# Gates stored 32 tokens at a time, picks made first, small transfers by way of DRAM, the last modulation column one pair behind its load

## The chip, the cores and the metric

The kernel runs on one NeuronCore of a Trainium2 chip. The metric is the device time of one execution in microseconds, the median of several runs. TensorE multiplies matrices, VectorE (DVE) and ScalarE (ACT) work element by element, GpSimd (POOL) mainly issues gathers here, and SyncE (SP) issues the other transfers. Each engine takes its instructions in order. An instruction that waits for a transfer holds up all that stand behind it on its engine, and the same holds for the queue of transfers that an engine issues.

## What is computed

One layer of a diffusion backbone over 512 tokens of width 1024. A token mixer of two gated scans comes first. Then comes a retrieval layer, cut here to its core:

```python
q = (t @ w_query).reshape(PEER_BLOCK, PEER_HEADS, 2, PEER_DQ // 2)
s1 = jnp.einsum('thd,nd->thn', q[:, :, 0], k1)
s2 = jnp.einsum('thd,nd->thn', q[:, :, 1], k2)
v1, i1 = lax.top_k(s1, PEER_TOPK)
v2, i2 = lax.top_k(s2, PEER_TOPK)
...
top_s, pos = lax.top_k(cand_s, PEER_TOPK)
idx = jnp.take_along_axis(cand_i, pos, axis=-1)
g = jax.nn.softmax(top_s, axis=-1)
act = jax.nn.gelu(jnp.einsum('thkd,td->thk', expert_u[idx], t))
return jnp.einsum('thk,thkd->td', (g * act), expert_v[idx])
```

For each token, 8 heads pick 16 of 16384 experts each. An expert is one row of U and one row of V. The result times a modulation vector g2 = silu(c) @ w_ada + b, plus the residual, is normalised and written.

## The kernel before

**Two ways to the same sum.** Tokens stand in four blocks of 128. For block 3 the picked rows are fetched with indirect gathers (tile erow, `fetched`, L1199): 128 rows of U, multiplied with h on VectorE (L1229), and 128 rows of V, added up in yg (L1242). For blocks 0 to 2 (384 tokens) the kernel computes all 16384 experts densely: `hidden` (L1138) makes gelu(U h) for one pair of 128 experts at a time, 64 pairs in all, `gated` (L1162) multiplies by a gate matrix that is zero where an expert was not picked, and `combine` (L1189) adds the pair's V rows into six accumulators y. The last 16 tokens of the 384 are left out of `hidden` (368 columns instead of 384); their products come from 16 more fetched rows, the s rows (L1223), whose sums sdots go through a gelu (L1225) and are put into the tile act by eight small transfers (L1227).

**Float32 in three products.** Each operand is split into a high and a low part: ScalarE writes the high part (uh, vh, ah; L1134, L1181), VectorE the rest (ul, vl, al; L1135, L1182), and TensorE runs three matmuls for each (`mm3`, L139 to L141). The tile pH holds `hidden`, y `combine`, pG the gates. A pair's `combine` is 36 matmuls of 512 columns, its `hidden` 48 of 368. V rows (tile vr, 1 MB a pair) are loaded and split by `load_split` (L1125), U rows (ur) too.

**The gate matrix.** `gate_block` (L1114) builds gates for 8 tokens at a time, 48 groups: VectorE makes one-hot factors (L1093 to L1104), TensorE multiplies them (pG, L1110), ScalarE copies them into the tile stage (L1111), and when 16 tokens are full SP stores the stage to Gd in DRAM (L1121), 24 stores of 1 MB. `gated` reads Gd back for four pairs at a time into Gn (L1169, 1.5 MB).

**Order.** The queries come first and with them the picks, four blocks of `picks` (L1022), then the gate stage with `hidden` and fetched rows mixed in; the constants ROWS say how many fetched rows go with each gate group, with each half of a pair that has `hidden`, and with each half of one that has none. By the end of the gate stage 32 pairs of `hidden` are asked for, so the main loop has 32 pairs with `hidden` and `combine`, then 29 with `combine` alone, and a tail of three. The gelus of 28 pairs are kept in DRAM (Hd, stored at L1155, loaded back at L1161). When the last `hidden` is done its memory is freed for a new pool, `vring`. From there on the V rows of pairs alternate between the two pools, and `mods_last` (L251) runs: it loads silr once (L255) and eight columns wg of the g2 weights (L259), each followed by a product on VectorE (L260), one per pair.

VectorE's order within the loops is settled by the scheduler when the program is built, from the order of the code and its estimates of when inputs are ready.

Of the kernel before, what the change touches and what calls it, by code (L numbers as in the profile page):

```python
# [19 lines left out]
D = 1024  # L20
# [11 lines left out]
class Net:  # L32
# [218 lines left out]
    def mods_last(self, pool):  # L251
# [680 lines left out]
class Peer:  # L932
# [10 lines left out]
    GT = 16  # L943
# [4 lines left out]
    ROWS = (0.85, 2.85, 0.83)  # L948
# [73 lines left out]
    def picks(self, w, b):  # L1022
# [12 lines left out]
        for s in range(2):  # L1035
# [11 lines left out]
        key = self.key = (self.n.q0[0][:, 256:512].rearrange("p (s h k) -> p s h k", s=2, h=8) if b == 2 else  # L1047
                          w.tile([128, 2, 8, 16], F32, name="key"))
# [114 lines left out]
    def gated(self, n, pool, vpool, bufs, mark=None, home=None):  # L1163

        nc = self.nc
        NG, NU = self.TD // self.GT, self.TU // self.GT
        if 2 * n % self.GN == 0:
            self.Gn = pool.tile([128, NG, self.GN, self.GT], F32, name="Gn", bufs=2)
            nc.sync.dma_start(self.Gn, self.Gd[:, :, 2 * n:2 * n + self.GN, :].rearrange("g m n t -> m g n t"))  # L1169
# [4 lines left out]
        nc.scalar.activation(g4[:, :, NU:], gates[:, :, NU:], AF.Copy)  # L1174
        with self.tc.issue_after(mark) if mark else ExitStack():
            nc.vector.tensor_tensor(g4[:, :, :NU], g4[:, :, :NU], gates[:, :, :NU], op=OP.mult)
# [20 lines left out]
    def fetched(self, w, ring, y):  # L1197
# [64 lines left out]
    def run(self, es, out):  # L1262
# [5 lines left out]
        self.Hd = dp.tile([self.SPILL, 128, 2, self.TU], F32, name="Hd")  # L1268
        kept, out_to = self.AHEAD, self.AHEAD + self.SPILL
        seq = [*range(kept), *range(out_to, 64), *range(kept, out_to)]  # L1270
        self.shared = False
        self.gel, self.last = {}, 2 * seq[-1]
# [5 lines left out]
        with ExitStack() as e0:  # L1278
# [5 lines left out]
            with ExitStack() as e1:  # L1284
                w = e1.enter_context(tc.tile_pool(name="top", bufs=1, side="right", reuse_waits="tile"))
# [5 lines left out]
                self.iota2 = w.tile([128, 128, 2], BF, name="iota2")  # L1291
# [8 lines left out]
                with tc.tile_pool(name="wq", bufs=1, reuse_waits="tile") as wp:  # L1300
# [10 lines left out]
                    nc.gpsimd.tensor_copy(self.iota2, n.iota_row[:, :, None].to_broadcast([128, 128, 2]))  # L1311
# [6 lines left out]
                self.ixs = fp.tile([128, self.SH], I32, name="ixs")  # L1318
                self.dots, self.act = (n.q0[0][:, i:i + 128] for i in (0, 128))
# [3 lines left out]
                def index():  # L1323
# [149 lines left out]
```

## Time and profile before

| | us |
|---|---|
| runs of the kernel | 1751.51, 1754.22, 1760.5; median 1754.22 |
| profiled execution | 1756.08, of it 1754.0 in the span |
| TensorE, VectorE, ScalarE, GpSimd busy | 1666.8, 1449.4, 830.5, 500.1 |
| gate matmuls (pG), first to last start | 689.6 to 923.3 |
| combine matmuls (y), first start | 948.5 |
| mean granted clock of TensorE | 0.98 of full speed |

A matmul's modelled duration overlaps the next one's, so TensorE can be "busy" nearly all the time without running at its peak. A better measure is the number of matmuls that start in a window, set against the shortest steady distance between two. The granted clock shows in windows where TensorE had to wait.

### The profile page before, as it was taken

The numbers are of one execution on the slowest core, as the hardware profiler recorded it, in microseconds if no ns is written. First come the engines' busy times: TensorE is split into PE (matmuls) and PEld (weight loads), VectorE is DVE, ScalarE is ACT, GpSimd is POOL, SyncE is SP. The second block draws the span as 40 slices with busy tenths as digits, with TensorE's granted clock in tenths as the row PEclk, the third lists the DMA queues.
The fourth block names the chain that finished last, engine by engine and source line by source line (L and its number), as shares of the span: only waits on it lengthen the run. The fifth ranks groups of instructions, "written<-read, shape, count | busy, mean of one in ns | idle before, by whom it ended". The sixth has DMA issues, their size and how long they took to land. (4 is left out here: it accounts for less than half of the span.)

```text
span 1754.0 us, 27581 instructions
## 1 busy us (share of the span) xinstructions
PE 1666.8 (95%) x10440; PEld 1456.8 (83%) x10440; DVE 1449.4 (83%) x2824; ACT 830.5 (47%) x1413; POOL 500.1 (29%) x327
## 2 busy tenths in 40 slices
PE   6999999989999999989998999999999998999995
PEld 3888877877788999988997989999999997788884
DVE  6688988877989999979996698788778876778677
ACT  4667677655233365757663244333333332234231
POOL 0000000000043012212383575565556551323310
PEclk8999999989999999999999999999999999999998
DMA  8345445133322247878899989999999989999962
GB/s 315 128 145 160 131 144 181 55 156 136 146 85 73 97 155 272 323 265 295 334 324 384 363 338 360 348 329 348 352 319 355 345 282 346 329 321 336 327 214 96
DMA packets 155687, 439.13 MB, mean 250 GB/s; under 512 B 13105, under 2 KB 69777, under 8 KB 135074
## 3 DMA queue, kind: packets, MB, share of 16 engines
q1 hardware_dynamic: 114322, 289.94, 47.7%
q0 software_dynamic: 40400, 145.34, 22.7%
q8 instruction: 81, 1.33, 0.3%
q10 hardware_dynamic: 832, 2.11, 0.3%
q14 instruction: 52, 0.43, 0.1%
HBM read 388.93 MB, written 48.39 MB: 249 GB/s over the span
## 5 line engine op out<-in xcount | busy, mean ns | idle before, releaser
L141 PE MATMUL pH<-hh,ul 128*128 128x368 f32 x1024 | 340.9, 333 | 4.0 <-DVE ul L1135 4.0
L139 PE MATMUL pH<-hh,uh 128*128 128x368 f32 x1024 | 340.4, 332 | 3.2 <-ACT gels L1153 2.5
L140 PE MATMUL pH<-hl,uh 128*128 128x368 f32 x1024 | 338.1, 330 | 0.0
L139 PE MATMUL y<-vh,ah 128*128 128x512 f32 x756 | 297.0, 394 | 13.2 <-ACT ah L1181 7.2
L1214 POOL DMA_INDIRECT erow<-in_v_dram,ix x128 | 231.2, 1806 | 255.8 <-DVE yg L1242 168.0
L141 PE MATMUL y<-vh,al 128*128 128x512 f32 x756 | 295.8, 392 | 3.6 <-DVE al L1182 3.6
L140 PE MATMUL y<-vl,ah 128*128 128x512 f32 x756 | 296.8, 393 | 0.1
L1214 POOL DMA_INDIRECT erow<-in_u_dram,ix x128 | 202.6, 1583 | 254.6 <-DVE erow L1229 141.9
L1134 ACT ACTIVATE uh<-ur 128x1024 fp32r<-128x1024 f32 x128 | 135.3, 1059 | 209.6 <-PE pH L140 181.4
L1135 DVE TENSOR_TENSOR vl<-vr,vh 128x1024 fp32r<-128x1024 f32 x126 | 153.3, 1222 | 95.6 <-ACT vh L1134 95.5
L1134 ACT ACTIVATE vh<-vr 128x1024 fp32r<-128x1024 f32 x126 | 132.4, 1055 | 186.8 <-PE y L141 128.0
L139 PEld LDWEIGHTS pH<-hh,uh 128*128 128x128 f32 x1024 | 193.2, 189 | 5.3 <-ACT gels L1153 2.8
L141 PEld LDWEIGHTS pH<-hh,ul 128*128 128x128 f32 x1024 | 193.0, 189 | 5.4 <-DVE ul L1135 5.4
L140 PEld LDWEIGHTS pH<-hl,uh 128*128 128x128 f32 x1024 | 193.3, 189 | 1.3
L139 PEld LDWEIGHTS y<-vh,ah 128*128 128x128 f32 x756 | 143.7, 190 | 43.6 <-ACT ah L1181 8.5
L1135 DVE TENSOR_TENSOR ul<-ur,uh 128x1024 fp32r<-128x1024 f32 x128 | 154.5, 1216 | 30.7 <-ACT uh L1134 30.7
L141 PEld LDWEIGHTS y<-vh,al 128*128 128x128 f32 x756 | 143.3, 190 | 35.5 <-DVE al L1182 5.1
L140 PEld LDWEIGHTS y<-vl,ah 128*128 128x128 f32 x756 | 143.2, 189 | 29.2 <-DVE vl L1135 0.4
L1242 DVE SCALAR_TENSOR_TENSOR yg<-erow,q,yg 128x1024 f32<-128x1024 f32 x127 | 162.5, 1279 | 0.5
L1229 DVE SCALAR_TENSOR_TENSOR erow<-erow,h 128x1024 f32<-128x1024 f32 x128 | 151.4, 1219 | 1.8 <-DMA erow<-in_u_dram,ix 1.8
L139 PE MATMUL pc<-hTh,wh 128*128 128x512 f32 (+1 forms) x304 | 109.6, 360 | 0.3 <-ACT G L379 0.3
L140 PE MATMUL pc<-hTl,wh 128*128 128x512 f32 (+1 forms) x304 | 108.2, 356 | 0.0
(407 smaller groups left out, 3040.9 us busy)
## 6 DMA issues: line engine op xcount, KB each, us to landing
ur<-in_uT_dram SPq DMA_DIRECT2D x64, 1024.0 KB, 8.2
vr<-in_vd_dram SPq DMA_DIRECT2D x64, 1024.0 KB, 7.7
Gd<-stage SPq DMA_DIRECT2D x24, 1024.0 KB, 6.7
Gn<-Gd SPq DMA_DIRECT2D x16, 1536.0 KB, 15.5
wraw<-in_w_cf_dram SPq DMA_DIRECT2D x24, 512.0 KB, 4.0
wada<-in_w_ada_dram SPq DMA_DIRECT2D x48, 256.0 KB, 3.1
Hd<-gels SPq DMA_DIRECT2D x28, 368.0 KB, 5.6
gel<-Hd SPq DMA_DIRECT2D x28, 368.0 KB, 6.0
```

Source lines behind the costliest of these rows:

```text
L139: mm(out, lh, rh, start=start, stop=False)
L140: mm(out, lh, rl, start=False, stop=False)
L141: mm(out, ll, rh, start=False, stop=stop)
L1134: nc.scalar.activation(hi, raw[:, e], AF.Copy)
L1135: self.mark = nc.vector.tensor_tensor(lo, raw[:, e], hi, op=OP.subtract).ins
L1214: nc.gpsimd.indirect_dma_start(out=e, out_offset=None, in_=a["v" if src == "v" else "u"], in_offset=bass.IndirectOffsetOnAxis(ap=ix[:, j:j ...
L1229: nc.vector.scalar_tensor_tensor(e, e, 1.0, h2, op0=OP.mult, op1=OP.mult, accum_out=dots[:, j:j + 1])
L1242: nc.vector.scalar_tensor_tensor(y, e, act[:, j:j + 1], y, op0=OP.mult, op1=OP.add)
```

## The change

It has five parts.

1. GT goes from 16 to 32. A stage holds the gates of 32 tokens, Gd is stored in 12 pieces of 2 MB, and each contiguous piece that Gn reads is 1024 bytes instead of 512. Since 368 is no multiple of 32, VectorE's gate product is split in two (352 and 16 columns for each expert).
2. The picks of blocks 0 and 1 are made ahead of the gate stage, and the pool they work in is closed before the gate stage's pool opens. The constant iota2 moves to another pool.
3. ROWS changes: more fetched rows per gate group and per pair without `hidden`, fewer per pair with it.
4. The index transfers (eight on GpSimd's queue) and the transfers of sdots (eight on ScalarE's) become two each on GpSimd's queue: one to DRAM, one back in the other layout.
5. In `mods_last` the product of a column is emitted one pair after its load, and the first column comes one pair later. The V rows of pair 32 go to the old pool; vring is first used by pair 33.

```diff
     def mods_last(self, pool):
...
-        for j in range(8):
-            w = pool.tile([128, D], F32, name="wg2")
-            nc.sync.dma_start(w, a["w_g2"][j])
-            nc.vector.scalar_tensor_tensor(w, w, 1.0, sr, op0=OP.mult, op1=OP.mult, accum_out=m2[:, j:j + 1])
-            yield
+        for j in range(9):
+            if j:
+                nc.vector.scalar_tensor_tensor(w, w, 1.0, sr, op0=OP.mult, op1=OP.mult, accum_out=m2[:, j - 1:j])
+            if j < 8:
+                w = pool.tile([128, D], F32, name="wg2")
+                nc.sync.dma_start(w, a["w_g2"][j])
+                yield
...
-    GT = 16
+    GT = 32
...
-    ROWS = (0.85, 2.85, 0.83)
+    ROWS = (0.95, 2.7, 0.93)
...
-            nc.vector.tensor_tensor(g4[:, :, :NU], g4[:, :, :NU], gates[:, :, :NU], op=OP.mult)
+            for t in [(slice(0, NU),)] + [(NU, slice(0, rest))] * (rest > 0):
+                at = (slice(None), slice(None), *t)
+                nc.vector.tensor_tensor(g4[at], g4[at], gates[at], op=OP.mult)
...
-                    for q in range(128 // SH):
-                        nc.scalar.dma_start(act[128 - SH:128, q * SH:(q + 1) * SH], sdots[q * SH:(q + 1) * SH, :])
+                    nc.gpsimd.dma_start(self.sad.rearrange("q t k -> (q t) k"), sdots)
+                    nc.gpsimd.dma_start(act[128 - SH:128, :].rearrange("t (q k) -> t q k", k=SH),
+                                        self.sad.rearrange("q t k -> t q k"))
...
-                for q in range(128 // SH):
-                    nc.gpsimd.dma_start(self.ixs[q * SH:(q + 1) * SH, :], self.ix[128 - SH:128, q * SH:(q + 1) * SH])
+                nc.gpsimd.dma_start(self.ixd.rearrange("q t k -> t q k"),
+                                    self.ix[128 - SH:128, :].rearrange("t (q k) -> t q k", k=SH))
+                nc.gpsimd.dma_start(self.ixs, self.ixd.rearrange("q t k -> (q t) k"))
...
-                with tc.tile_pool(name="bd", bufs=1, reuse_waits="tile") as bp:
-                    for i, _ in enumerate(self.picks(w, 0)):
+                for b in (0, 1):
+                    for i, _ in enumerate(self.picks(w, b)):
                         if i % 2:
                             more(0.5)
-                    more(0.5)
+                top.close()
+                with tc.tile_pool(name="bd", bufs=1, reuse_waits="tile") as bp:
...
-                vp, pools, first = None, [w], 0
+                vp, first = None, 64
...
-                    else:
+                    elif i > first + 1:
                         next(g2, None)
                     fetch(rate)
-                    v = self.rows(m, pools[(i - first) % len(pools)])
+                    v = self.rows(m, vp if vp and i > first + 1 and (i - first) % 2 == 0 else w)
```

The change moves instructions at three places. The first is ScalarE in the middle of the gate stage, from the last gate copies before the gelu of sdots; `q` is the tile that act lies in. Before:

```order
L1111 ACTIVATE stage<-pG 128x128x4 x4
L1225 ACTIVATE sdots<-sdots 128x16
L1227 DMA q_4768<-sdots 16x16 x2
L1153 ACTIVATE gels<-pH 128x368
L1227 DMA q_4768<-sdots 16x16 x6
L1134 ACTIVATE uh<-ur 128x1024
L1153 ACTIVATE gels<-pH 128x368
```

After the change:

```order
L1113 ACTIVATE stage<-pG 128x128x4 x2
L1230 ACTIVATE sdots<-sdots 128x16
L1102 ACTIVATE ohg<-oh_8556,g2f 128x128 x4
L1113 ACTIVATE stage<-pG 128x128x4 x2
L1102 ACTIVATE ohg<-oh_8664,g2f 128x128 x4
L1136 ACTIVATE uh<-ur 128x1024
```

ScalarE's queue holds no transfer there any more. They are now in GpSimd's, between row fetches (u rows, then v rows of block 3):

```order
L1348 DMA ixd<-ix 16x8x16
L1350 DMA ixs<-ixd 128x16
L1219 DMA erow<-in_u_dram,ixs 128x1024 x16
L1219 DMA erow<-in_u_dram,ix 128x1024 x5
L1231 DMA sad<-sdots 128x16
L1232 DMA q_4768<-sad 16x8x16
L1219 DMA erow<-in_u_dram,ix 128x1024 x11
```

The transfers of sdots stand behind the first five u rows and ahead of the other eleven. The second place is SP's queue at the end of the gate stage, from the last stores of gates to the first read of Gn. Before:

```order
L1121 DMA Gd<-stage 128x2048
L1130 DMA ur<-in_uT_dram 128x2048
L1155 DMA Hd<-gels 128x736
L1121 DMA Gd<-stage 128x2048
L1130 DMA vr<-in_vd_dram 128x2048
L1169 DMA Gn<-Gd 128x24x128
L1155 DMA Hd<-gels 128x736
```

After the change:

```order
L1123 DMA Gd<-stage 128x4096
L1157 DMA Hd<-gels 128x736
L1132 DMA ur<-in_uT_dram 128x2048
L1132 DMA vr<-in_vd_dram 128x2048
L1172 DMA Gn<-Gd 128x12x256
```

The last store is twice as large, and the last store of Hd and one load of U rows now stand ahead of the read of Gn. On TensorE, 108 matmuls of `hidden` stand between the last gate matmul and the first `combine` before, 144 after. The third place is the start of the pairs without `hidden`. On SP's queue before, vr_14973 is pair 31, vr_15035 pair 32, vr_15098 pair 33:

```order
L1130 DMA vr_14973<-in_vd_dram 128x2048
L1130 DMA vr_15098<-in_vd_dram 128x2048
L1169 DMA Gn_15296<-Gd_5199 128x24x128
L1130 DMA vr_15221<-in_vd_dram 128x2048
L1161 DMA gel_15108<-Hd_5200 128x2x368
L1161 DMA gel_15171<-Hd_5200 128x2x368
L255 DMA silr_15030<-sild_73 128x1024
L259 DMA wg2_15032<-in_w_g2_dram 128x1024
L1130 DMA vr_15035<-in_vd_dram 128x2048
```

After the change vr_14953 is pair 31, vr_15012 pair 32, vr_15077 pair 33:

```order
L1132 DMA vr_14953<-in_vd_dram 128x2048
L1132 DMA vr_15012<-in_vd_dram 128x2048
L1172 DMA Gn_15280<-Gd_5199 128x12x256
L1132 DMA vr_15138<-in_vd_dram 128x2048
L1163 DMA gel_15087<-Hd_5200 128x2x368
L1163 DMA gel_15148<-Hd_5200 128x2x368
L255 DMA silr_15070<-sild_73 128x1024
L262 DMA wg2_15072<-in_w_g2_dram 128x1024
L1132 DMA vr_15077<-in_vd_dram 128x2048
```

The rows that stand last, behind silr and the first wg, were pair 32's and are now pair 33's. On VectorE at the same place, before (al_15050 belongs to pair 32, al_15113 to pair 33):

```order
L1182 TENSOR_TENSOR al_15050<-gel_14509,ah_15049 128x768
L260 SCALAR_TENSOR_TENSOR wg2_15032,m2_987<-wg2_15032,silr_15030 128x1024
L1135 TENSOR_TENSOR vl_15101<-vr_15098,vh_15100 128x1024
L1135 TENSOR_TENSOR vl_15038<-vr_15035,vh_15037 128x1024
L1135 TENSOR_TENSOR vl_15042<-vr_15035,vh_15041 128x1024
```

After the change al_15028 belongs to pair 32 and al_15093 to pair 33:

```order
L1187 TENSOR_TENSOR al_15028<-gel_14489,ah_15027 128x768
L1137 TENSOR_TENSOR vl_15015<-vr_15012,vh_15014 128x1024
L259 SCALAR_TENSOR_TENSOR wg2_15072,m2_987<-wg2_15072,silr_15070 128x1024
L1137 TENSOR_TENSOR vl_15019<-vr_15012,vh_15018 128x1024
L1235 SCALAR_TENSOR_TENSOR erow_14944,q00_4768<-erow_14944,h2_3_5113 128x1024
L1235 SCALAR_TENSOR_TENSOR erow_14947,q00_4768<-erow_14947,h2_3_5113 128x1024
L1137 TENSOR_TENSOR vl_15080<-vr_15077,vh_15079 128x1024
L1137 TENSOR_TENSOR vl_15084<-vr_15077,vh_15083 128x1024
L1181 TENSOR_TENSOR gel_14622<-gel_14622,Gn_15022 128x2x352
L1181 TENSOR_TENSOR gel_14622<-gel_14622,Gn_15022 128x2x16
L1235 SCALAR_TENSOR_TENSOR erow_14950,q00_4768<-erow_14950,h2_3_5113 128x1024
L1187 TENSOR_TENSOR al_15093<-gel_14622,ah_15092 128x768
```

The first product with wg now stands between the two halves of pair 32's vl, not ahead of both.

## Rows read from the trace of the kernel before

**Rows 1.** Windows: busy (xstarted) of PE, PEld, DVE, ACT, POOL; PEclk, DMA share, GB/s.

```profile
500.00:925.00 425.00, 410.19 (x3064) 385.20 (x3063) 407.56 (x1217) 242.31 (x470) 129.02 (x76) 0.99 0.66 230
940.00:960.00 20.00, 13.76 (x53) 11.34 (x54) 14.55 (x18) 6.15 (x12) 7.61 (x6) 0.83 1.05 397
960.00:1440.00 480.00, 479.71 (x2497) 436.98 (x2496) 392.03 (x447) 174.93 (x246) 272.39 (x170) 1.00 0.94 340
1450.00:1470.00 20.00, 13.95 (x52) 10.99 (x51) 8.09 (x9) 4.72 (x7) 1.68 (x1) 0.83 0.84 316
1470.00:1520.00 50.00, 45.66 (x193) 36.68 (x192) 40.50 (x44) 17.24 (x23) 15.30 (x10) 0.97 0.98 354
1520.00:1700.00 180.00, 179.74 (x792) 148.16 (x791) 134.29 (x146) 65.32 (x84) 55.08 (x32) 1.00 0.93 317
```

**Rows 2.** Waits of VectorE, 500 to 925: total us, times, longest.

```profile
DVE ul L1135 <- ACT uh L1134: 14.9, 6, 9.3
```

**Rows 3.** Timeline of ScalarE, 764 to 772.

```profile
764.24 7.28 ACTq L1227 DMA_DIRECT2D q<-sdots  x6
771.57 1.06 ACT L1134 ACTIVATE uh<-ur 128x1024 fp32r<-128x1024 f32 x1 [6.87 <-DMA q<-sdots]
```

**Rows 4.** Timeline of TensorE around the gate's end.

```profile
923.32 0.42 PE L139 MATMUL pH<-hh,uh 128*128 128x368 f32 x1
942.03 0.33 PE L141 MATMUL pH<-hh,ul 128*128 128x368 f32 x1
948.51 0.80 PE L139 MATMUL y<-vh,ah 128*128 128x512 f32 x1 [6.15 <-ACT ah L1181]
```

**Rows 5.** Timeline of SP's queue, 924 to 934.

```profile
924.18 0.32 SPq L1121 DMA_DIRECT2D Gd<-stage  x1
933.88 0.38 SPq L1169 DMA_DIRECT2D Gn<-Gd  x1
```

**Rows 6.** Timeline of ScalarE, 946.

```profile
946.60 0.59 ACT L1174 ACTIVATE gel<-Gn 128x32 f32<-128x32 f32 x4 [5.62 <-DMA Gn<-Gd]
```

**Rows 7.** Timeline of TensorE, 1464.

```profile
1464.30 2.92 PE L139 MATMUL y<-vh,ah 128*128 128x512 f32 x6 [6.05 <-ACT vh L1134]
```

**Rows 8.** Timeline of SP's queue, 1449 to 1450.

```profile
1449.63 0.42 SPq L259 DMA_DIRECT2D wg<-in_w_g_dram  x1
1450.10 0.43 SPq L1130 DMA_DIRECT2D vr<-in_vd_dram  x1
```

**Rows 9.** Timeline of ScalarE, 1450 to 1463.

```profile
1450.81 0.35 ACT L1174 ACTIVATE gel<-Gn 128x32 f32<-128x32 f32 x2 [3.42 <-DMA Gn<-Gd]
1463.19 2.95 ACT L1134 ACTIVATE vh<-vr 128x1024 fp32r<-128x1024 f32 x3 [7.93 <-DMA vr<-in_vd_dram]
```

**Rows 10.** Timeline of VectorE, 1460.

```profile
1460.78 1.23 DVE L260 SCALAR_TENSOR_TENSOR wg<-wg,silr 128x1024 f32<-128x1024 f32 x1 [12.39 <-DMA wg<-in_w_g_dram]
```

**Rows 11.** Issues of transfers: KB each, median us to landing.

```profile
ur<-in_uT_dram SPq DMA_DIRECT2D x64, 1024.0 KB, 8.2
Gd<-stage SPq DMA_DIRECT2D x24, 1024.0 KB, 6.7
Gn<-Gd SPq DMA_DIRECT2D x16, 1536.0 KB, 15.5
ixs<-ix POOLq DMA_DIRECT2D x8, 1.0 KB, 4.6
```

**Rows 12.** Timeline of GpSimd, 656.

```profile
656.61 1.16 POOL L1214 DMA_INDIRECT erow<-in_u_dram,ixs  x1 [5.37 <-PE pH L141]
```

**Rows 13.** Instructions of line 1223.

```profile
L1223 DVE SCALAR_TENSOR_TENSOR erow<-erow,yg x16: 1212/1216/1222, 676.0 to 761.0; 128x1024 f32<-128x1024 f32 x16
```

**Rows 14.** Groups of VectorE by form, 480 to 1760.

```profile
L1242 DVE SCALAR_TENSOR_TENSOR yg<-erow,q,yg 128x1024 f32<-128x1024 f32 x127 | 162.5, 1279 | 0.5
L1238 DVE TENSOR_TENSOR q<-q,gp 128x16 f32<-128x16 f32 x8 | 1.3, 168 | 0.0
```

**Rows 15.** Waits of VectorE, 1440 to 1540.

```profile
DVE wg L260 <- DMA wg<-in_w_g_dram: 17.4, 4, 12.4
```

More of the change, by code (lines that the diff above doesn't have):

```diff
@@ L1166, in gated @@
         NG, NU = self.TD // self.GT, self.TU // self.GT
+        rest = self.TU % self.GT
         if 2 * n % self.GN == 0:
@@ L1173, in gated @@
         gates = self.Gn[:, :, m:m + 2, :].rearrange("p g n t -> p n g t")
-        nc.scalar.activation(g4[:, :, NU:], gates[:, :, NU:], AF.Copy)
+        nc.scalar.activation(g4[:, :, NU, rest:], gates[:, :, NU, rest:], AF.Copy)
         with self.tc.issue_after(mark) if mark else ExitStack():
-            nc.vector.tensor_tensor(g4[:, :, :NU], g4[:, :, :NU], gates[:, :, :NU], op=OP.mult)
+            for t in [(slice(0, NU),)] + [(NU, slice(0, rest))] * (rest > 0):
+                at = (slice(None), slice(None), *t)
+                nc.vector.tensor_tensor(g4[at], g4[at], gates[at], op=OP.mult)
         if home:
@@ L1268, in run @@
         self.Hd = dp.tile([self.SPILL, 128, 2, self.TU], F32, name="Hd")
+        self.ixd = dp.tile([128 // self.SH, self.SH, self.SH], I32, name="ixd")
+        self.sad = dp.tile([128 // self.SH, self.SH, self.SH], F32, name="sad")
         kept, out_to = self.AHEAD, self.AHEAD + self.SPILL
@@ L1271, in run @@
         self.shared = False
-        self.gel, self.last = {}, 2 * seq[-1]
+        self.gel, self.keys, self.last = {}, {}, 2 * seq[-1]
         pers = es.enter_context(tc.tile_pool(name="pers", bufs=1, reuse_waits="tile"))
@@ L1284, in run @@
             with ExitStack() as e1:
-                w = e1.enter_context(tc.tile_pool(name="top", bufs=1, side="right", reuse_waits="tile"))
+                top = e1.enter_context(ExitStack())
+                w = top.enter_context(tc.tile_pool(name="top", bufs=1, side="right", reuse_waits="tile"))
                 ps = e1.enter_context(tc.tile_pool(name="qps", bufs=1, space=PSUM, reuse_waits="tile"))
@@ L1318, in run @@
                 self.ixs = fp.tile([128, self.SH], I32, name="ixs")
+                self.iota2 = fp.tile([128, 128, 2], BF, name="iota2")
+                nc.gpsimd.tensor_copy(self.iota2, n.iota_row[:, :, None].to_broadcast([128, 128, 2]))
                 self.dots, self.act = (n.q0[0][:, i:i + 128] for i in (0, 128))
@@ L1322, in run, with index @@
                 more(1.0)
-                def index():
-                    nc.vector.scalar_tensor_tensor(self.ix, self.key[:, 0].rearrange("p h k -> p (h k)"), 128.0,
-                                                   self.key[:, 1].rearrange("p h k -> p (h k)"), op0=OP.mult, op1=OP.add)
+                def index(b):
+                    k0, k1 = (self.keys[b][:, s].rearrange("p h k -> p (h k)") for s in range(2))
+                    nc.vector.scalar_tensor_tensor(self.ix, k0, 128.0, k1, op0=OP.mult, op1=OP.add)
                 for i, _ in enumerate(self.picks(w, 2)):
@@ L1328, in run @@
                         more(0.5)
-                index()
-                key2 = self.key
+                index(2)
                 nc.vector.memset(self.act[96:128], 1.0)
@@ L1345, in run @@
                         more(0.5)
-                index()
+                index(3)
                 choice.close()
@@ L1366, in run @@
                         assert b < 2 or self.shared
-                        kg = self.picks_on_partitions(bp, ps, key2 if b == 2 else self.key, self.g[:, b])
-                        following = self.picks(w, 1) if b == 0 else iter(())
-                        for i, _ in enumerate(self.gate_block(bp, ps, b, kg)):
+                        kg = self.picks_on_partitions(bp, ps, self.keys[b], self.g[:, b])
+                        for _ in self.gate_block(bp, ps, b, kg):
                             at += 1
-                            if i >= 2 and i % 2 == 0:
-                                next(following, None)
                             fetch(self.ROWS[0])
                             more(first + (out_to - first) * at / groups - asked)
-                        for _ in following:
-                            pass
             with ExitStack() as e1:
@@ L1421, in run @@
                         for j in range(3)]
-                    vs.append(self.rows(m, pools[(64 - self.TAIL + c - first) % 2], home and home[:2]))
+                    vs.append(self.rows(m, (vp, w)[(64 - self.TAIL + c - first) % 2], home and home[:2]))
                     acts.append(self.gated(m, w, w, self.TAIL - 1, mark, home and home[2]))
```

7 lines of the change are left out of this document (2 added, 5 removed).

## Prediction, made before the changed kernel ran

> **What bounds the kernel now.** I read the stages first, in windows of the span [rows 1]. From 960 to 1440 and from 1520 to 1700 us TensorE starts matmul after matmul with no gap: 792 starts in 180 us are one per 0.227 us for 512 columns, the granted clock is 1.00, and nothing but less TensorE work would shorten these stretches. From 500 to 925 us VectorE is the full engine, busy for 407.6 of 425 us. What is left to win lies at the seams, where TensorE starts too few matmuls and the granted clock drops: 940 to 960 (0.83), 1450 to 1470 (0.83) and 1470 to 1520 (0.97). So I price the change seam by seam and ask of every other edit whether it makes one of the full stretches longer.
>
> In the gate stage VectorE hardly waits for anything but ScalarE's split of the up rows: 14.9 us in six waits, one of them 9.3 [rows 2]. The long one has a cause that can be read: ScalarE issues small transfers of sdots for 7.28 us and reaches the next split only at 771.57 [rows 3].
>
> At the gate's end the last gate matmuls stop at 923.3. TensorE has up-projection matmuls until 942.2, then waits 6.15 us for ah [rows 4]. That chain runs over DRAM: the last store of gates is issued at 924.18, the read of the first Gn is held until it has landed, at 933.88 [rows 5], and ScalarE gets Gn at 946.60 [rows 6]. The first combine matmul starts 1.9 us later.
>
> At the end of the hidden work TensorE waits 6.05 us until 1464.30, for vh of pair 32 [rows 7]. These rows of V were issued only at 1450.10, behind silr and the first wg [rows 8], and came at 1463.19 [rows 9]. VectorE meanwhile stands 12.39 us in the product with that wg [rows 10].
>
> **The change, part by part.** *ScalarE's eight transfers go to GpSimd as two.* In the new order of ScalarE one-hot work and splits follow the gelu at once, so I take the 9.3 us of [rows 2] as gone. GpSimd now waits for the gelu and then for one landing between the two transfers; a transfer of that size landed in 4.6 us [rows 11], so the queue is held some 5 us and the result is there after about 9. The product that uses it first comes after the fifth u row, and VectorE works off rows one per 5 us. The stage fetches 45.6 rows in its 235 us, five of them ahead, so the fetches held behind in GpSimd's queue have 25 us of cover; without it up to 9 us would fall on VectorE. The index transfers, now two in a row, are later by one landing at most; the fetch that needs them starts at 656.61 [rows 12] and the first fetched row is used at 676.0 [rows 13], 19 us of cover. I cost both at nothing.
>
> *More rows in the gate stage.* 0.95 instead of 0.85 for each of 48 groups are 4.8 rows, and the new VectorE order indeed holds five more of them before its last gate product. At 1.28 us each [rows 14] they cost 6.4 us on the full engine. So the gate ends 9.3 − 6.4 = 2.9 us earlier (bounds 0 and 9.3): last gate matmul at 920.4. All picks in front of the gates reorder VectorE work of unchanged size; they were almost all there already. Nothing.
>
> *The seam at 942.* The new order of TensorE has 144 up matmuls instead of 108 between the last gate matmul and the first combine. 108 took 18.9 us, so 0.17 each; 144 take 24.5, up to 944.9. The 36 extra matmuls are work brought forward, worth 36 × 0.17 = 6.1 us, as far as the data doesn't come later. The data: the last store is 2 MB instead of 1. One took 933.88 − 924.18 = 9.7 us beside much other traffic (median 6.7 [rows 11]). The second megabyte costs at least 2.7 us at the 397 GB/s of this window [rows 1], at most another 6.7; I take 4. The first Gn took 12.7 us (933.88 to 946.60). Its pieces double to 1024 bytes. Per 1024 KB, Gn's median is 10.3 us against 8.2 for ur [rows 11]; if the longer pieces brought it to ur's rate it would save 2.6 of 12.7, if not, nothing. I take 1. So Gn is there at 946.6 − 2.9 + 4 − 1 = 946.7 and the first combine starts at 948.6, as before, with 6.1 us less work behind it: **−6.1 us** (bounds: +0.6 with the gate's 2.9 and Gn's 1 lost and the store at 6.7, which makes the start 6.7 later; −10 with the data so early that the start follows the 144 at 944.9).
>
> The Trainium skill (page "DMA: Bandwidth & Descriptors", section Specifications) puts the smallest transfer for full rate at 512 bytes. By that rule doubling pieces of 512 bytes gives nothing, the term of 1 us would fall away and the gain here would be 5.1 instead of 6.1. The rows lean against it, 10.3 against 8.2 us per 1024 KB, but they differ in more than their pieces.
>
> *The seam at 1458.* Pair 32 now reads V into the old pool, so its load stands long before silr. Its vh, vl and al are ready by 1457: in ScalarE's new order ah stands behind the copy out of the next Gn, which arrived at 1450.81 [rows 9], so al ends near 1453. The wait of 6.05 is gone. But VectorE still meets the first wg product between vl of the pair's two halves, and wg is issued at the same place in SP's queue, so VectorE is held until 1460.78 as now [rows 10]. Operations over 1024 columns take 1.2 to 1.3 us [rows 10, 14]. Product and second vl end at 1463.3; the second half of pair 32 is due at 1458.2 + 18 × 0.227 = 1462.3: 1 us of waiting. Then two rows, two vl and the gate product take VectorE to 1469.3, ah to 1470.1, one row and al to 1471.3, while pair 33 is due at 1467.4: 3 us. So **the stall is smaller and one pair later**. Now 1450 to 1470 holds 52 starts, 11.8 us of work, so 8.2 are lost: 6.05 of waiting and 2.1 of half clock after it. I put 1 + 3 + 2 = 6 in its place, a gain of 2.2. From 1470 to 1520, 193 starts are 43.8 us, 6.2 lost. There VectorE waits 17.4 − 12.4 = 5.0 us for the other wg [rows 15], and SP holds later loads behind it. With each product one pair behind its load these waits end, but a late Gn stays possible: I count 3.3 of the 6.2 as won. Together **−5.5 us** (bounds −1 and −11).
>
> *Combine-only pairs.* Rows per pair go from 1.66 to 1.86: 0.26 us more VectorE work. The second, 16-column product is nearest to a row of 0.17 us [rows 14]; its bounds are nothing and the 1.2 of a whole 1024-column operation. VectorE now works 134.3 of 180 us or 6.1 per pair of 8.17 and goes to 6.5. The DMA engines are at a share of 0.93 and 317 GB/s; 0.2 × 512 KB per pair adds 13 GB/s, to 0.97. TensorE hides it: nothing, as long as both stay under the pair's time. Pairs with hidden work get 5.4 rows instead of 5.7, in a stretch set by TensorE: nothing.
>
> **Sum.** −6.1 − 5.5 = −11.6 on the profiled execution's 1756.1 gives 1744.5. That execution lies 1.9 above the median of the runs, so I give 1743.
>
> **Rivals.** (a) *One seam gives nothing.* If VectorE's hold on the first wg costs pair 33 as much as pair 32 lost, only the 6.1 stay: 1748. For it: VectorE's order still has the product ahead of both vl of pair 33. Against it: pair 32 runs 8 us of work in the meantime. If instead the 2 MB store eats the 36 matmuls, 5.5 stay: 1749. (b) *The combine-only phase turns from TensorE to DMA or VectorE* (the other side). The DMA share is 0.98 from 1470 to 1520 already, with wg in flight. If the rows make a pair cost 8.9 instead of 8.17 us, 29 pairs cost 21 us: 1754.2 − 11.6 + 21 = 1764, slower. It decides from a share of about 1.0, that is from 340 GB/s; 340 were moved at 0.94 before 1440, which speaks against it. (c) *Both seams close.* If Gn comes early and VectorE is not held, 10 + 11 = 21 us go: 1733. Against it: silr, wg and V are still issued together at 1450 with the DMA engines full.
>
> **How the numbers follow.** Forecast 0.50 (own range 1738 to 1748), (a) 0.22 (1746 to 1752), (c) 0.18 (1729 to 1737), (b) 0.10 (1755 to 1770). 0.5%, 8.8 us, is about what a measurement of this kernel can tell from no change: faster means under 1745.4. Of the forecast about 0.38 lies there, with (c) and a little of (a) 0.58; slower, above 1763, is half of (b) and mishaps not listed, 0.07; the rest 0.35. The range from 1732 to 1753 leaves out (b) and the lower half of (c).
>
> **What would show it.** Right: no wait of VectorE over 3 us for ScalarE's split near 770; first combine near 948, but with 36 more up matmuls done; no wait at pair 32's start, one of 2 to 4 us at pair 33; 8.17 us per pair up to 1700. Wrong: a Gn read held over 15 us by the last store; VectorE waiting for fetched rows in the gate stage; gaps at every pair after 1520.

## The result and the profile after

The changed kernel takes 1744.54 us (median of 15 runs, 1740.1 to 1750.82), the kernel before 1754.28 in the runs beside it: a ratio of 0.9939, 95% interval 0.9924 to 0.9954. It is 10.7 us faster by the ratio. Timed once more on another chip (e8 below) it gave 0.9922, interval 0.9905 to 0.994. The forecast of 1743 was close. But the sum that led to it does not hold. The gate stage gave three times what it was to give and lost it again at the seam at 942, which so gave next to nothing. The seam at 1458 gave what it was to give or more, but not by the edit that was to bring it.

Windows of the changed kernel, over the same stretches as [rows 1], columns as there:

```profile
500.00:925.00 425.00, 416.47 (x3116) 392.85 (x3115) 415.11 (x1206) 245.94 (x473) 138.35 (x78) 1.00 0.67 241
940.00:960.00 20.00, 11.10 (x39) 8.73 (x40) 14.65 (x22) 6.31 (x11) 8.10 (x6) 0.73 1.03 406
960.00:1440.00 480.00, 480.00 (x2490) 437.17 (x2489) 381.63 (x455) 174.02 (x242) 245.50 (x161) 1.00 0.90 329
1450.00:1470.00 20.00, 18.68 (x83) 15.13 (x82) 17.31 (x24) 8.17 (x11) 6.73 (x4) 1.00 0.98 372
1470.00:1520.00 50.00, 46.96 (x200) 38.04 (x199) 41.33 (x50) 15.35 (x20) 16.78 (x12) 0.97 0.99 363
1520.00:1700.00 180.00, 178.34 (x784) 146.35 (x783) 137.22 (x169) 65.07 (x86) 51.99 (x32) 1.00 0.87 307
```

From 500 to 925 VectorE is busier than before. The seam at 942 is worse, with a clock of 0.73 where it was 0.83. The seam at 1458 is better, with 83 starts for 52. The steady stretches start within 8 matmuls of what they did.

**The gate stage.** The waits of VectorE in the changed kernel, 500 to 925 (total, times, longest), to be set against [rows 2]:

```profile
DVE ul L1137 <- ACT uh L1136: 7.4, 5, 2.8
```

The wait of 9.3 is gone. To weigh it I take each execution from its own first up matmul (pH) to its own last gate matmul, so that chance in the stages ahead drops out. The first up matmul came at 488.3 before and at 484.0 here, in a stage that the change doesn't touch, and at 489.3 in the second execution of the same kernel. Window over just this stretch, of the kernel before:

```profile
488.30:923.30 435.00, 418.91 (x3100) 391.67 (x3099) 416.49 (x1281) 245.33 (x474) 132.78 (x77) 0.99 0.65 226
```

and of the changed kernel:

```profile
484.00:910.40 426.40, 416.60 (x3098) 390.06 (x3098) 417.95 (x1282) 245.29 (x472) 136.52 (x77) 1.00 0.65 232
```

VectorE's work is the same within 1.5 us, and TensorE starts the same matmuls. The idle time falls from 435.0 − 416.5 = 18.5 to 426.4 − 418.0 = 8.4 us. The stage is 8.6 us shorter.

**The seam at 942.** Timeline of SP's queue in the changed kernel, from the last store of gates to the first read (compare [rows 5]):

```profile
912.66 0.32 SPq L1123 DMA_DIRECT2D Gd<-stage  x1
920.02 0.32 SPq L1157 DMA_DIRECT2D Hd<-gels  x1
920.44 0.67 SPq L1132 DMA_DIRECT2D ur<-in_uT_dram  x1
921.21 0.51 SPq L1132 DMA_DIRECT2D vr<-in_vd_dram  x1
926.27 0.38 SPq L1172 DMA_DIRECT2D Gn<-Gd  x1
```

of ScalarE, where it has Gn (compare [rows 6]):

```profile
943.45 0.59 ACT L1177 ACTIVATE gel<-Gn 128x32 f32<-128x32 f32 x4 [4.54 <-DMA Gn<-Gd]
```

and of TensorE, its first combine matmul (compare [rows 4]):

```profile
946.62 0.80 PE L139 MATMUL y<-vh,ah 128*128 128x512 f32 x1 [11.91 <-ACT ah L1186]
```

The last gate matmul started at 910.4. The store was issued 2.3 us later, the read 13.6 after that, ScalarE had Gn at 943.45, 17.2 us after the read, and the combine began 3.2 later: 36.2 us in all. Before, the same chain was 0.9, 9.7, 12.7 and 1.9, together 25.2 ([rows 4 to 6]). So the longer chain takes back all that the gate stage won: counted from the first up matmul, the first combine comes at 462.6 us where it came at 460.2. In exchange 36 more up matmuls are done. Counted to the last up matmul, where that exchange is settled, the change has won 0.7 us (960.7 for 961.4).

**The seam at 1458.** Waits of TensorE in the changed kernel, 1430 to 1540:

```profile
PE y L139 <- ACT ah L1186: 4.6, 3, 2.6
PE y L141 <- DVE al L1187: 1.1, 2, 0.7
```

The wait of 6.05 for vh at pair 32 [rows 7] is gone. Pair 33 waits 1.3 us at 1462.68. The longest, 2.6 at 1498.23, comes a few pairs later, after ScalarE has waited 10.1 us for a Gn. VectorE's waits for wg fell from 17.4 to 8.4 us [rows 15]. Timeline of SP's queue in the changed kernel at the first wg (compare [rows 8]):

```profile
1445.80 0.43 SPq L262 DMA_DIRECT2D wg<-in_w_g_dram  x1
1446.28 1.18 SPq L1132 DMA_DIRECT2D vr<-in_vd_dram  x2
```

and of VectorE at the product with it (compare [rows 10]):

```profile
1453.91 1.23 DVE L259 SCALAR_TENSOR_TENSOR wg<-wg,silr 128x1024 f32<-128x1024 f32 x1 [2.44 <-DMA wg<-in_w_g_dram]
```

The product starts 8.1 us after the load was issued, before 11.2. From the last up matmul to the last combine matmul the kernel takes 279.5 us, before 286.0. So 6.5 of the 7.2 us by which the last combine comes nearer to the first up matmul lie behind the last up matmul. Of the 11.3 us between the two spans 4.3 lie ahead of the first up matmul, where e8 shows chance.

### The profile page after: what moved, and what is told of

It reads as the page before. It is cut to its first block, busy times and chain, and to the rows that moved or that the text cites. A ratio compares the mean times of both kernels' runs of the same rounds, so it can differ in the third digit from the quotient of the medians.

```text
span 1742.7 us, 27586 instructions
## 1 busy us (share of the span) xinstructions
PE 1657.3 (95%) x10440; PEld 1450.2 (83%) x10440; DVE 1455.1 (83%) x2888; ACT 833.2 (48%) x1413; POOL 486.9 (28%) x323
## 5 line engine op out<-in xcount | busy, mean ns | idle before, releaser
L1219 POOL DMA_INDIRECT erow<-in_v_dram,ix x128 | 214.0, 1672 | 268.6 <-DVE yg L1248 142.4
L1219 POOL DMA_INDIRECT erow<-in_u_dram,ix x128 | 206.8, 1616 | 228.5 <-DVE erow L1235 127.1
```

The source lines that it names most:

```text
L1219: nc.gpsimd.indirect_dma_start(out=e, out_offset=None, in_=a["v" if src == "v" else "u"], in_offset=bass.IndirectOffsetOnAxis(ap=ix[:, j:j ...
```

## The experiments

Every kernel was timed beside the kernel before on the same chip, in five rounds. e1 to e4 shared a chip, e5 to e8 another, e9 to e11 a third; e12 ran on a fourth. This table gives the ratio of the medians, and from each profile four distances that start at the execution's own first up matmul: to the last gate matmul, to the first combine matmul, to the last up matmul and to the last combine matmul.

| kernel | ratio, interval | last gate | first combine | last up | last combine |
|---|---|---|---|---|---|
| before | 1 | 435.0 | 460.2 | 961.4 | 1247.4 |
| changed | 0.9939 [0.9924, 0.9954] | 426.4 | 462.6 | 960.7 | 1240.2 |
| e8 changed, again | 0.9922 [0.9905, 0.994] | 427.0 | 463.4 | 960.9 | 1236.8 |
| e12 part 4 alone | 0.9962 [0.9949, 0.9976] | 427.3 | 452.6 | 954.2 | 1244.0 |
| e9 part 2 alone | 0.9943 [0.9923, 0.9963] | 428.9 | 454.2 | 956.1 | 1240.7 |
| e10 parts 2 and 1 | 0.9944 [0.9923, 0.9965] | 431.8 | 464.6 | 959.1 | 1240.6 |
| e6 part 5 alone | 1.0014 [1.0001, 1.0027] | 436.1 | 462.4 | 963.0 | 1250.5 |
| e1 without part 1 | 0.9945 [0.9928, 0.9962] | 432.0 | 466.2 | 960.3 | 1240.1 |
| e4 without part 3 | 0.9928 [0.9909, 0.9946] | 425.1 | 457.9 | 952.7 | 1231.6 |
| e3 without part 4's sdots | 0.9945 [0.9927, 0.9963] | 431.5 | 467.5 | 965.1 | 1240.2 |
| e7 without part 5 | 0.9933 [0.992, 0.9946] | 426.8 | 462.6 | 959.1 | 1237.9 |
| e2 store in two | 0.9925 [0.9906, 0.9944] | 431.5 | 467.1 | 963.2 | 1239.2 |
| e5 store in two, first Gn on GpSimd | 0.9912 [0.9898, 0.9927] | 425.6 | 455.4 | 953.5 | 1230.6 |
| e11 as e5, without part 3 | 0.9961 [0.9945, 0.9977] | 425.8 | 451.3 | 959.2 | 1243.0 |

**One part undone.** e1, with GT at 16 again:

```diff
-    GT = 32
+    GT = 16
```

> The changed kernel with GT back at 16 (24 stores of 1 MB, pieces of 512 bytes), all else changed. My theory: in the changed kernel TensorE waited 11.9 us for the first gates because the last 2 MB store took 13.6 us until the read of Gn could be issued, and the read then 17.2 us; half a store costs some 4 us less, so the first combine matmul starts near 943 instead of 946.6, and the ratio to the kernel before is 0.992. Rival 1, the volume: the DMA engines are full around the gate's end and move the same bytes whatever their division; first combine within 1.5 us of 946.6, ratio 0.994. Rival 2, the pieces: reads of Gn in 512-byte pieces take 15.5 us instead of 13.0 in the median, the waits of pairs 32 to 40 grow, ratio 0.996 or more.

e3, with ScalarE's eight transfers back:

```diff
-                    nc.gpsimd.dma_start(self.sad.rearrange("q t k -> (q t) k"), sdots)
-                    nc.gpsimd.dma_start(act[128 - SH:128, :].rearrange("t (q k) -> t q k", k=SH),
-                                        self.sad.rearrange("q t k -> t q k"))
+                    for q in range(128 // SH):
+                        nc.scalar.dma_start(act[128 - SH:128, q * SH:(q + 1) * SH], sdots[q * SH:(q + 1) * SH, :])
```

> The changed kernel with the eight transfers of sdots back on ScalarE's queue. My theory: the wait of 9 us near 765 comes back, the gate stage ends 8 to 11 us later (last gate matmul near 920), but TensorE waits for Gn anyway, so the first combine comes at most 3 us later and the ratio is 0.994 to 0.996. Rival: the end of the gate stage sets the first combine as before, it comes 8 us or more later and the ratio is 0.998 or more.

e4, with the old ROWS:

```diff
-    ROWS = (0.95, 2.7, 0.93)
+    ROWS = (0.85, 2.85, 0.83)
```

> The changed kernel with ROWS of before. My theory: the gate stage ends some 5 us earlier, near 905, which gives nothing at the first combine (within 2 us of 946.6), and the combine-only pairs keep 8.17 us either way: ratio 0.993 to 0.995. Rival: more rows per combine-only pair cost time on VectorE or the DMA engines, so with fewer the stretch from 1520 to 1700 is 2 us shorter and the ratio 0.992 or less.

e7, with the old mods_last and the old alternation of pools (part 5 as in the diff of the change, backwards):

> The changed kernel with part 5 undone (product right behind its load, V rows of pair 32 in vring). My theory: the wait of some 6 us at pair 32 is back, the ratio is 0.9975 to 1.0, about 6 us above the changed kernel. Rival: the other four parts hold most of the gain, ratio 0.996 or less.

None of the four can be told from the changed kernel; all intervals overlap. So with the other parts in place none of parts 1, 3, 5, nor the transfers of sdots in part 4, carries the gain alone. Of the four theories those of e1 and e7 failed: in e1 the first combine came later, not earlier, and in e7 the ratio did not rise. Those of e3 and e4 had the ratio about right and the steps not: in e3 the gate stage ends 5 us later, not 8 to 11, in e4 only 1.3 us earlier, not 5, and the first combine comes 4.7 us earlier where it was to stay. In e3 ScalarE's transfers stand in the gate stage again, and the longest wait of VectorE for the split is 2.4 us there, not 9.3. That was the first sign that the stall is not a matter of the transfers alone. In e7 TensorE waits 4.13 us at pair 32 again, and the time is the same.

e8, the changed kernel once more, as a measure of chance:

> The changed kernel once more, for a second trace and a ratio on the same chip as the three others. Of the 11.3 us between the two spans 4.4 lie ahead of the first up matmul, in a stage that the change doesn't touch. If that is chance, the second trace has the first up matmul elsewhere between 483 and 489; if the change causes it, near 484 again. In both cases the wait for the first Gn is 9 to 13 us and the ratio 0.994.

The first up matmul came at 489.3, so the 4.4 us ahead of it are chance. The wait for the first Gn was 12.1 us, as expected.

**One part alone.** e6, the kernel before with part 5:

```diff
-        for j in range(8):
+        for j in range(9):
+            if j:
+                nc.vector.scalar_tensor_tensor(w, w, 1.0, sr, op0=OP.mult, op1=OP.mult, accum_out=m2[:, j - 1:j])
...
-                    v = self.rows(m, pools[(i - first) % len(pools)])
+                    v = self.rows(m, vp if vp and i > first + 1 and (i - first) % 2 == 0 else w)
```

> The kernel before with part 5 of the change alone (product one pair behind its load, V rows of pair 32 in the old pool). My theory: nearly all of the change's gain is this seam; TensorE's wait of 6.05 us at pair 32 falls under 2 us, from pair 31 to pair 40 it saves 6 to 7 us, ratio 0.995 to 0.997. Rival: the seam got shorter because gates are read in longer pieces and fewer rows come with the pairs ahead of it; then part 5 alone saves under 3 us, ratio 0.998 or more.

Nothing, or a loss of 2.5 us at the edge of what can be told. Timeline of TensorE in e6, at pair 32:

```profile
1459.61 0.79 PE L140 MATMUL y<-vl,ah 128*128 128x512 f32 x1 [4.06 <-DVE vl L1137]
```

and of ScalarE, at the next two reads of Gn:

```profile
1501.54 0.35 ACT L1176 ACTIVATE gel<-Gn 128x32 f32<-128x32 f32 x2 [9.32 <-DMA Gn<-Gd]
...
1532.82 0.23 ACT L1176 ACTIVATE gel<-Gn 128x32 f32<-128x32 f32 x1 [14.26 <-DMA Gn<-Gd]
```

Part of the wait at pair 32 comes back at once, as a wait for vl, and ScalarE waits 9 and 14 us for the next two Gn. The longest wait for Gn there was 9.0 before.

e9, the kernel before with part 2 alone: all picks ahead of the gates, GT, ROWS, mods_last and all transfers as before.

```diff
-                    for i, _ in enumerate(self.picks(w, 0)):
+                for b in (0, 1):
+                    for i, _ in enumerate(self.picks(w, b)):
...
-                        following = self.picks(w, 1) if b == 0 else iter(())
-                        for i, _ in enumerate(self.gate_block(bp, ps, b, kg)):
+                        for _ in self.gate_block(bp, ps, b, kg):
...
-                            if i >= 2 and i % 2 == 0:
-                                next(following, None)
```

> The kernel before with part 2 alone (all picks ahead of the gates). So far each part undone alone (GT, the transfers of sdots, ROWS, part 5) left nearly the whole gain, and part 5 alone gained nothing. The stretch where the gain lies runs from pair 32 to pair 42: 128 us in the changed kernel and without part 5, 135 to 137 in the kernel before and with part 5 alone, counted from the 1056th combine matmul to the 1512th. Theory L, the load: the DMA engines are full there, and either the longer pieces of Gn (share 0.90 instead of 0.95 in the loop ahead) or the rows moved from the loop to the gate stage relieve them; then part 2 alone has neither, 134 us or more for the stretch and a ratio of 0.999 or more. Theory P, the order: picks first gives the scheduler another order up to the end, and that order holds the gain; then the stretch takes 130 us or less and the ratio is 0.996 or less.

Part 2 alone gives as much as the whole change, within the interval. Neither theory holds: the stretch took 134.1 us, as theory L had it, with the ratio of theory P. So part 2's gain lies ahead of that stretch (which begins in pair 29, not 32). The reason can be read at ScalarE's eight transfers. Timeline of VectorE before, at its longest wait (ScalarE at the same time is in [rows 3]):

```profile
762.17 1.22 DVE L1135 TENSOR_TENSOR ul<-ur,uh 128x1024 fp32r<-128x1024 f32 x1
772.66 1.23 DVE L1135 TENSOR_TENSOR ul<-ur,uh 128x1024 fp32r<-128x1024 f32 x1 [9.27 <-ACT uh L1134]
773.80 0.28 DVE L1075 CAST gp<-pkT 128x128 bf16<-128x128 f32 x1
774.00 1.22 DVE L1093 TENSOR_TENSOR oh<-iota,kT 128x2048 bf16<-128x2048 bf16 x1
```

and of ScalarE in e9, where the transfers stand as before:

```profile
765.10 0.46 ACT L1070 ACTIVATE kT<-pkT 128x128 bf16<-128x128 f32 x2
765.41 0.25 ACT L1228 ACTIVATE sdots<-sdots 128x16 f32<-128x16 f32 x1
765.70 6.25 ACTq L1230 DMA_DIRECT2D q<-sdots  x7
...
772.64 1.06 ACT L1134 ACTIVATE uh<-ur 128x1024 fp32r<-128x1024 f32 x1 [0.16 <-issue]
```

and of VectorE in e9:

```profile
766.19 0.29 DVE L1075 CAST gp<-pkT 128x128 bf16<-128x128 f32 x1
766.39 1.22 DVE L1093 TENSOR_TENSOR oh<-iota,kT 128x2048 bf16<-128x2048 bf16 x1
...
772.21 0.42 DVE L1104 TENSOR_TENSOR ohg<-oh,gp 128x512 bf16<-128x512 bf16 x1
773.73 1.22 DVE L1135 TENSOR_TENSOR ul<-ur,uh 128x1024 fp32r<-128x1024 f32 x1 [1.09 <-ACT uh L1134]
```

In both, ScalarE issues transfers for some 7 us while a split of up rows stands behind them. Before, VectorE's next instruction is the one that needs this split. The one-hot work of the next gate block stands behind it, and its keys kT are copied only after the transfers. In e9 the keys are copied ahead of the transfers and the one-hot work stands ahead of the waiting subtraction. VectorE fills 766 to 772.5 with it and waits 1.1 us. Window of e9 from first up to last gate matmul:

```profile
484.60:913.50 428.90, 418.54 (x3098) 392.05 (x3098) 417.37 (x1281) 244.94 (x474) 107.93 (x77) 1.00 0.65 229
```

Work 417.4 for 416.5 us, idle 11.5 for 18.5. The waits for the split are 8.3 us in this stretch instead of 14.9.

e12 was the counter-test: if the gain is this wait, then taking away the transfers alone must give it too.

```diff
-                    for q in range(128 // SH):
-                        nc.scalar.dma_start(act[128 - SH:128, q * SH:(q + 1) * SH], sdots[q * SH:(q + 1) * SH, :])
+                    nc.gpsimd.dma_start(self.sad.rearrange("q t k -> (q t) k"), sdots)
+                    nc.gpsimd.dma_start(act[128 - SH:128, :].rearrange("t (q k) -> t q k", k=SH),
+                                        self.sad.rearrange("q t k -> t q k"))
```

(and the index transfers as in the change)

> The kernel before with part 4 alone: index transfers and transfers of sdots as two each on GpSimd's queue; picks, ROWS, GT and mods_last as before. ScalarE's order is that of before without its eight transfers, the split of the up rows stands right behind the gelu of sdots. Theory (what part 2 won is the wait of 9.3 us for ScalarE's split in the gate stage; whoever takes it away gets the same): the wait near 770 is gone, VectorE's waits for the split in the stage fall from 14.9 to 6 to 9 us, the stage from first up matmul to last gate matmul takes about 429 us instead of 435.0, and the ratio is 0.993 to 0.996, as with part 2 alone. Rival 1 (part 2 won something else, the transfers are worth nothing): the stage stays at 433 to 436 us, ratio 0.999 to 1.001. Rival 2 (the transfers move the wait to GpSimd: fetched rows come late behind the two transfers of sdots): VectorE waits over 3 us for erow between 765 and 800, ratio 0.998 to 1.003.

The wait is gone here too. Timeline of ScalarE in e12:

```profile
762.06 0.22 ACT L1225 ACTIVATE sdots<-sdots 128x16 f32<-128x16 f32 x1 [2.67 <-DVE erow L1223]
762.74 1.06 ACT L1134 ACTIVATE uh<-ur 128x1024 fp32r<-128x1024 f32 x1 [0.47 <-PE pH L140]
```

The split now stands right behind the gelu. Window of e12 from first up to last gate matmul:

```profile
487.90:915.20 427.30, 418.14 (x3101) 390.81 (x3099) 415.66 (x1280) 244.96 (x474) 131.83 (x72) 1.00 0.65 230
```

Idle 11.6 us, the stage 427.3, as short as in the changed kernel. VectorE's waits for the split fell to 9.0 us there, and from 765 to 800 it waits for no fetched row, so rival 2 did not come. The ratio of 0.9962 lies just outside what was expected. Its interval overlaps that of part 2 alone. So either part takes away the same wait, and they do not add: the full change ends the stage only 0.3 to 2.5 us ahead of the one or the other. Over all fourteen traces the stage takes 435.0 and 436.1 us in the two that have a wait of over 9 us for the split of up rows (before and e6), and 425.1 to 432.0 in the twelve that have none over 4.

e10, parts 2 and 1 (e9 with GT at 32):

> The kernel before with parts 2 and 1 (picks first, GT 32), old ROWS, old transfers, old part 5. Theory L: the longer pieces alone relieve the DMA engines, the loop's share falls to 0.93, the stretch from the 1056th to the 1512th combine matmul takes 130 us or less and the ratio is 0.995. Rival: neither picks nor pieces, but the rows or the transfers of sdots carry the gain; the stretch stays at 134 us or more and the ratio at 0.998 or more.

By the ratio GT at 32 neither adds nor takes. The first combine comes 10.4 us later than in e9 (464.6 for 454.2), with 36 more up matmuls done, and the way from the first to the last combine is 10.5 us shorter (776.0 for 786.5). The stretch of the forecast took 130.6 us, just over the 130 of theory L. GT at 32 without part 2 was not tried.

**The way behind the last up matmul.** It is the difference of the last two columns of the table. The kernels fall into four groups by GT and ROWS:

| | old ROWS | new ROWS |
|---|---|---|
| GT 16 | before 286.0, e12 289.8, e9 284.6, e6 287.5 | e1 279.8 |
| GT 32 | e10 281.5, e4 278.9, e11 283.8 | changed 279.5, e8 275.9, e7 278.8, e3 275.1, e2 276.0, e5 277.1 |

So the gain of the seam at 1458 goes with parts 1 and 3: with neither the way takes 284.6 us or more, with both 279.5 or less, with one of them it lies between or near. The two traces of the changed kernel are 3.6 us apart, so only the first and the last group are told apart. Part 5 has no share: it is in e6 and not in e7. In the seven traces with the new ROWS SP issues two loads of V rows right behind the first wg, in the seven with the old ROWS one. Whether that is how part 3 works was not tested, and neither part was tried alone on the kernel before.

**The seam at 942.** e2 splits the store: the eight experts of the first Gn go to a tensor of their own, so that its read has to wait for a last store of 128 KB instead of 2 MB.

```diff
-                    nc.sync.dma_start(self.Gd[b * (128 // GT) + q], stage)
+                    nc.sync.dma_start(self.G0[b * (128 // GT) + q], stage[:, :self.GN])
+                    nc.sync.dma_start(self.Gd[b * (128 // GT) + q, :, self.GN:], stage[:, self.GN:])
```

> The changed kernel, in which each stage is stored in two parts: the 8 rows of experts that the first Gn reads go first, 128 KB, into a DRAM tile of their own; the first Gn no longer waits for the rest of the last store. My theory (the store holds Gn): Gn is issued behind the load of V that stands ahead of it, near 921.7 instead of 926.3, lands 4 to 6 us earlier, the first combine starts near 942 and the ratio is 0.991. Rival, the volume: the DMA engines are full, Gn still lands near 943 and the ratio stays 0.994.

e5 is e2 with this first read on GpSimd's queue, ahead of the main loop:

```diff
+                nc.gpsimd.dma_start(self.Gn, self.G0.rearrange("g m n t -> m g n t"))
```

> As the run with the stage stored in two parts (the 8 rows of experts of the first Gn in a DRAM tile of their own), and the first Gn is read by GpSimd's queue, no longer behind the last store of Hd and the loads of U and V rows on SP's. In that run Gn was issued 15 us after the last gate matmul although its data had been stored, since SP's queue stood at Hd, which waits for ScalarE's gelu. My theory, the queue: Gn is issued within 7 us of the last gate matmul, lands 6 to 9 us earlier, the first combine then waits for V and comes 4 us or more earlier (measured from the first up matmul: 458 or less instead of 462.7), ratio 0.991. Rival, the volume: between the gate's end and the first combine the DMA engines move 400 GB/s, so whatever is issued first delays the rest; first combine within 2 us of now, ratio 0.994.

Timeline of SP's queue in e2:

```profile
920.61 0.32 SPq L1123 DMA_DIRECT2D G<-stage  x1
920.98 0.44 SPq L1124 DMA_DIRECT2D Gd<-stage  x1
927.77 0.32 SPq L1158 DMA_DIRECT2D Hd<-gels  x1
928.19 0.92 SPq L1133 DMA_DIRECT2D ur<-in_uT_dram  x1
929.20 0.76 SPq L1133 DMA_DIRECT2D vr<-in_vd_dram  x1
933.21 0.38 SPq L1174 DMA_DIRECT2D Gn<-G  x1
```

Waits of SP's queue in e2, 915 to 936:

```profile
SPq L1158 <- ACT gels L1156: 14.5, 2, 8.3
SPq L1174 <- DMA Gd<-stage: 3.2, 1, 3.2
```

Timeline of GpSimd in e5:

```profile
920.43 1.08 POOL L1391 DMA_DIRECT2D Gn<-G  x1 [11.18 <-DMA G<-stage]
```

and of TensorE in e5, its first combine matmul:

```profile
942.45 0.80 PE L139 MATMUL y<-vh,ah 128*128 128x512 f32 x1 [7.16 <-ACT ah L1187]
```

In e2 the short store does not help: the read is issued 12.6 us after it. It stands behind Hd, which waits for ScalarE's gelu until 927.77, and then waits 3.2 us more for the store of the rest, of which it reads nothing. On GpSimd's queue it is issued when the short store has landed, 5.5 us after that was issued, and the first combine comes 11.7 us nearer to the first up matmul than in e2. Half of that, 5.9 us, is a gate stage that ended earlier in e5's trace. From the last gate matmul it is 29.8 us instead of 35.6, with 134 up matmuls in between instead of 144. e5 has the lowest time of all. Against the changed kernel on the same chip (e8, 0.9922) the intervals overlap, so its lead of about 2 us is not shown.

e11, e5 with the old ROWS, was meant to join the two lowest:

> The run with the first Gn read by GpSimd's queue, and with the old ROWS, the two variants that were at least as fast as the changed kernel. If the first combine then comes still earlier because fewer fetched rows share the DMA engines at the gate's end, the ratio is 0.989; if both gains are the same one, 0.991.

It is slower than e5, outside its interval. The first combine is the earliest of all. But ScalarE then waits 11.87 us for the second Gn, until 957.82, and TensorE 7.29 us behind it. And at 1456.42 VectorE has waited 8.46 us for a wg that stands ahead of pair 32's vl, and TensorE 4.06 for that vl.

## Why the number was right and the steps were not

**ScalarE's transfers (−9.3).** The wait went as forecast, and no wait for fetched rows took its place. e12 shows that part 4 alone takes it away.

**The picks, "Nothing": the step that failed.** "All picks in front of the gates reorder VectorE work of unchanged size; they were almost all there already. Nothing." The size is unchanged, 417.4 for 416.5 us. But the order of an engine that is full decides what stands in front of a wait. Here part 2 brings the next block's keys and one-hot work ahead of the stalled subtraction, and by itself it gives 10 us by the ratio, about as much as all five parts. In its trace 6.1 us are won at the last gate matmul and 6.7 at the last combine. I had read the wait of 9.3 from [rows 2, 3] and given it one cause, the transfers. It has two, and removing either is enough.

**More rows (+6.4).** Mis-sized: the stage came to 426.4 where the forecast was 435.0 − 2.9 = 432.1. Up to the last gate matmul VectorE did 12 of the products with V rows instead of 10, 2.6 us, where five more were counted, and one split less. Its work rose by 1.5 us in all. With the old ROWS (e4) the stage is 425.1, so the rows cost about 1.3 us in these traces.

**The seam at 942 (−6.1).** The 36 matmuls more were there, and the way from store to read grew by the 4 us of the forecast (13.6 − 9.7 = 3.9). The size of the store was only part of it: with stores of 1 MB (e1) it is still 11.7. What failed is "Gn −1": the first Gn took 17.2 us instead of 12.7. Window of the changed kernel while it was on its way:

```profile
926.00:944.00 18.00, 8.70 (x53) 8.40 (x51) 8.72 (x12) 5.04 (x9) 3.73 (x4) 0.81 1.03 399
```

and of the kernel before:

```profile
934.00:947.00 13.00, 7.84 (x46) 7.24 (x44) 5.84 (x7) 3.72 (x8) 3.99 (x4) 1.00 1.09 367
```

The DMA engines are full in both. In 18 us at 399 GB/s they moved 7.2 MB, in 13 at 367 only 4.8. With ur and vr issued 5 us ahead of Gn it shares them with more. The other traces bear this out. In the four kernels whose queue has only a vr between the last store and the read (before, e6, e9, e12) the read took 12.1 to 13.9 us, in the eight that have a ur there too 17.2 to 18.7. One of the eight is e1, so neither the longer pieces nor the larger store is the cause. No run moved the ur alone. Over the whole run Gn's median fell from 15.5 to 13.0 us, of which the same change with GT at 16 (e1) already has 0.5. From 960 to 1430 e9 moved 341 GB/s at a share of 0.94, e10 342 at 0.93, so the longer pieces gave little rate. That agrees with the rule of the Trainium skill cited in the prediction ("DMA: Bandwidth & Descriptors", Specifications). The seam as a whole, forecast to leave 6.1 us, left 0.7 at the last up matmul in the changed kernel and 0.5 in e8.

**The seam at 1458 (−5.5).** The size came true, the reason did not. Behind the last up matmul the changed kernel wins 6.5 us, e8 10.1. The edit priced here is part 5, and it is worth nothing: alone (e6) that way is 287.5 us for 286.0, undone (e7) 278.8 for 279.5, and the ratios say the same. The step that failed is "VectorE is held until 1460.78 as now": the first wg landed sooner, its product ran at 1453.91, and pair 33 waited 1.3 us, not 3. From 1437 to 1470 the DMA engines are at a share of 0.99 in the changed kernel, 0.90 before. The gain goes with parts 1 and 3, which the sum of this seam left out. That the number fits is luck. In part the waits come back: for Gn, 2.6 us at 1498.

**Combine-only pairs.** Right: 784 starts for 792, at a DMA share of 0.87. Rival (b) did not come. Rival (a) in its second form, the seam at 942 gives nothing, is what the traces show. By the sum that would be 1749. The measured 1744.5 is lower because the seam at 1458 gave more than its 5.5: the traces have 7.2 us (e8: 10.6) of the 11.6 forecast, the ratio has 10.7.

**Open.** What separates part 2 (0.9943) from part 4 (0.9962) alone: the intervals overlap. In the traces e12 takes 5.2 us longer than e9 behind the last up matmul; why was not found. Part 2 alone wins in the gate stage and the full change behind the last up matmul; that both come to the same ratio is not explained. Single executions differ by 3 us and more from first up to last combine (changed 1240.2, again 1236.8), so no step under that is settled by a trace.

## What to carry to other kernels

A stall on a full engine has two sides: what makes the awaited thing late, and what work stands behind the waiting instruction that could stand ahead of it. An edit that only reorders is worth zero only if no long wait lies in the stretch that it reorders, so compare the orders around the longest wait first. Where the DMA engines are full, a wait taken from one place can come back a few pairs later, as in e6: price it by what the engines have still to move, not by its own length. And two kernels with the same ratio need not have won at the same place: compare them at landmarks of their own work, here the last up matmul, before you name the part that did it.

## Not expected of the hardware

Around the seam the core moved 399 to 406 GB/s at a DMA share of 1.03, against 329 to 342 in the main loop at 0.90 to 0.95, so the loop's rate was not the most the engines gave. The same read left 12.6 us after its store on SP's queue and 5.5 us after it on GpSimd's, with the DMA engines almost as full in between (share 1.00 and 0.93).
